# Row sums of a 64 MB array: loads of 16 rows a partition in three buffers, a tapering last load, and a last row summed in three chained two-stream VectorE sums

## The chip, the cores and the metric

The kernel runs on one core of a Trainium2 chip. The metric is device time in microseconds (us). The span of a profile is shorter than that time by about 1.7 us: it goes from the first to the last instruction. All runs told here are of the fast state (granted clock 1.000).

## The reference

```python
def setup_inputs():
    batch, seq, dim = 32, 512, 1024
    return {"x": np.random.randn(batch, seq, dim).astype(np.float32)}

def reference(x):
    return np.sum(x, axis=-1).astype(np.float32)
```

That is 16,384 rows of 4 KB: 67.1 MB in, 64 KB out. Each of the 128 partitions gets 128 neighbouring rows (512 KB).

## The kernel before

The rows of a partition are loaded in 16 tiles of 8 rows (32 KB a partition, 4 MB in all) into four buffers. VectorE sums the first four rows of a tile in one instruction; ScalarE sums the other four with one copy and its accumulator each. The last tile comes in eight loads of one row, and the engines take turns. The code, cut to its core:

```python
    G = 8
    T = C // G                       # C = 128 rows a partition, T = 16 tiles
    DVE_N = 4
    x_t = x_flat.rearrange("(p t j) d -> t p j d", p=P, j=G)
    xpool = ctx.enter_context(tc.tile_pool(name="x", bufs=4))
    # ... res: one fp32 column a row, 128 x 128
    for t in range(T):
        xt = xpool.tile([P, G, D], x.dtype, tag="xt")
        c0 = t * G
        if t < T - 1:
            nc.sync.dma_start(out=xt, in_=x_t[t])
            reduce_cols_dve(xt[:, 0:DVE_N], c0, DVE_N)      # one tensor_reduce
            for j in range(DVE_N, G):
                reduce_col_act(xt[:, j], c0 + j)            # Copy with accum_out, in place
        else:
            for j in range(G):
                nc.sync.dma_start(out=xt[:, j], in_=x_t[t, :, j])
            for j in range(G):
                if j % 2 == 0:
                    reduce_col_act(xt[:, j], c0 + j)
                else:
                    reduce_cols_dve(xt[:, j], c0 + j, 1)
    nc.sync.dma_start(out=out2d, in_=res)
```

Of the kernel before, what the change touches and what calls it, by code (L numbers as in the profile page):

```python
# [1 line left out]

# [4 lines left out]


@with_exitstack
def kernel(  # L10
    ctx: ExitStack,
    tc: tile.TileContext,
    x: bass.AP,
    out: bass.AP,
):
    nc = tc.nc
    P = nc.NUM_PARTITIONS

    x_flat = x.flatten_outer_dims()
    R, D = x_flat.shape  # L20
    assert R % P == 0
    C = R // P

    G = 8
    assert C % G == 0
    T = C // G
    DVE_N = 4

    x_t = x_flat.rearrange("(p t j) d -> t p j d", p=P, j=G)

    out2d = out.rearrange("a (b c) -> (a b) c", c=C)

    xpool = ctx.enter_context(tc.tile_pool(name="x", bufs=4))
    rpool = ctx.enter_context(tc.tile_pool(name="res", bufs=1))

    res = rpool.tile([P, C], mybir.dt.float32)

    def reduce_col_act(xt_col, c):
        nc.scalar.activation(  # L39
            out=xt_col,  # L40
            in_=xt_col,
            func=mybir.ActivationFunctionType.Copy,
            accum_out=res[:, c : c + 1],
        )

    def reduce_cols_dve(xt_cols, c0, n):
        nc.vector.tensor_reduce(  # L47
            out=res[:, c0 : c0 + n],
            in_=xt_cols,
            axis=mybir.AxisListType.X,  # L50
            op=mybir.AluOpType.add,
        )

    for t in range(T):
        xt = xpool.tile([P, G, D], x.dtype, tag="xt")
        c0 = t * G
        if t < T - 1:
            nc.sync.dma_start(out=xt, in_=x_t[t])  # L58
            reduce_cols_dve(xt[:, 0:DVE_N], c0, DVE_N)
            for j in range(DVE_N, G):  # L60
                reduce_col_act(xt[:, j], c0 + j)
        else:
            for j in range(G):
                nc.sync.dma_start(out=xt[:, j], in_=x_t[t, :, j])
            for j in range(G):
                if j % 2 == 0:
                    reduce_col_act(xt[:, j], c0 + j)
                else:
                    reduce_cols_dve(xt[:, j], c0 + j, 1)

    nc.sync.dma_start(out=out2d, in_=res)


# [1 line left out]
_INS = ['x']  # L75
_OUTS = [((32, 512), 'float32')]


# [23 lines left out]
```

## Time and profile before

| | before |
|---|---|
| time, median | 165.24 us (165.18 to 165.28) |
| span of the profile | 163.7 us |
| VectorE, ScalarE busy | 43%, 43% |
| DMA in the chain of waits (the work that ended last, followed back) | 88% |
| last load lands, last row sum ends | 160.02, 161.26 us |

The page of the kernel before. The DMA row has one digit for each of 40 slices of the span, the mean busy share of the 16 DMA engines in tenths.

```profile
span 163.7 us, 243 instructions
DVE 71.0 (43%) x19; ACT 69.6 (43%) x129; POOL 0.2 (0%) x4
...
DMA  6999999999999999999999999999999999998980
...
DMA packets 3457, 67.18 MB, mean 410 GB/s; under 512 B 384, under 2 KB 512, under 8 KB 1536
```

The DMA engines are busy nearly all the time and the two summing engines less than half of it. So work on those engines costs time only where no load can hide it, which is at the end.

The timeline of the kernel before, VectorE alone. Columns: start, duration, engine, line, operation, output<-input, shapes, and in brackets the idle time before it and what ended that.

```profile
120.72 4.42 DVE L47 TENSOR_REDUCE res<-xt 128x4 f32<-128x4096 f32 x1 [5.30 <-DMA xt<-in_x_dram]
130.43 4.42 DVE L47 TENSOR_REDUCE res<-xt 128x4 f32<-128x4096 f32 x1 [5.29 <-DMA xt<-in_x_dram]
140.14 4.42 DVE L47 TENSOR_REDUCE res<-xt 128x4 f32<-128x4096 f32 x1 [5.29 <-DMA xt<-in_x_dram]
...
160.04 1.22 DVE L47 TENSOR_REDUCE res<-xt 128x1 f32<-128x1024 f32 x1 [1.28 <-DMA xt<-in_x_dram]
```

A load has landed when the last of the 16 DMA engines has marked its part of it complete. Each sum starts when its load has landed, so these starts are a clock for the stream: 9.71 us for 4,194,304 bytes is 432 GB/s. The last line is the tail: one row sum of 1.22 us after the last landing, and only then can the results be stored.

Below, a run of so many KB is the contiguous stretch that a load moves for one partition; each load has 128 runs, 8 for each DMA engine. The same kernel in two stretches, one with 32 KB runs and one with the 4 KB runs of the last tile. The last two columns are the DMA share and GB/s.

```profile
100.00:140.00 40.00, 17.68 (x4) 17.07 (x32) 0.00 (x0) 1.00 1.00 430
...
150.00:158.00 8.00, 6.99 (x4) 7.41 (x14) 0.00 (x0) 1.00 1.03 410
```

The DMA engines are equally busy in both, but move 5% less with the short runs. That is what a fixed cost for each run looks like.

### The profile page before, as it was taken

The page shows a single profiled execution, that of the slowest core. Times are in us where ns is not written, and L with a number is a line of the kernel's source. Part 1 is how long each engine was busy: PE and PEld are TensorE (multiplying, and loading weights), DVE is VectorE, ACT ScalarE, POOL GpSimd, SP SyncE. Part 2 cuts the span into 40 slices and gives each one's busy share as a digit, 9 for nine tenths or more (in the row PEclk, how much of TensorE's full clock was granted, in tenths as well). Part 3 has the DMA queues.
Part 4 walks back from the last instruction along what each step waited for, and adds up shares of the span by engine and source line. Part 5 has one row for each costly group of instructions (what it writes and reads, how often), then busy time and mean ns, then how long its engine had stood idle before and what let it go on. Part 6 is the DMA issues. An engine that isn't in the chain of part 4 may idle for free.

```text
span 163.7 us, 243 instructions
## 1 busy us (share of the span) xinstructions
DVE 71.0 (43%) x19; ACT 69.6 (43%) x129; POOL 0.2 (0%) x4
## 2 busy tenths in 40 slices
DVE  0006337091551907337090642808245190733952
ACT  3006337091551907336091642808145190733960
POOL 0000000000000000000000000000000000000000
DMA  6999999999999999999999999999999999998980
GB/s 200 432 432 440 416 448 416 416 432 424 424 424 440 416 448 424 416 456 424 432 442 416 448 416 424 448 432 432 432 424 448 416 424 448 424 432 364 407 349 16
DMA packets 3457, 67.18 MB, mean 410 GB/s; under 512 B 384, under 2 KB 512, under 8 KB 1536
## 3 DMA queue, kind: packets, MB, share of 16 engines
q1 hardware_dynamic: 3456, 67.18, 96.5%
q14 instruction: 1, 0.01, 0.0%
HBM read 67.11 MB, written 0.07 MB: 410 GB/s over the span
## 4 chain that ended last, share of the span: by engine, by line
DMA 88%; DVE 9%; SPq 1%; issue 0%
DMA xt<-in_x_dram 88%; DVE res L47 9%; SPq L58 1%
## 5 line engine op out<-in xcount | busy, mean ns | idle before, releaser
L47 DVE TENSOR_REDUCE res<-xt 128x4 f32<-128x4096 f32 (+1 forms) x19 | 71.0, 3745 | 90.3 <-DMA xt<-in_x_dram 90.3
L39 ACT ACTIVATE xt<-xt 128x1024 f32<-128x1024 f32 x64 | 66.8, 1044 | 89.6 <-DMA xt<-in_x_dram 89.6
L39 ACT ACTIVATION_READ_ACCUMULATOR xt<-xt 128x1 f32 x64 | 11.9, 187 | 0.0
L39 ACT ACT_TABLE_LOAD x1 | 1.3, 1283 | 0.7 <-PEq L86 0.7
L86 POOL MEMSET const-bfloat16-1.0<- 128x1 bf16 x1 | 0.1, 101 | 0.0
L86 POOL MEMSET const-uint8-127<- 128x1 uint8 x1 | 0.1, 101 | 0.0
L86 POOL MEMSET const-float32-0.0<- 128x1 f32 x1 | 0.1, 98 | 0.2 <-issue 0.2
L86 POOL MEMSET const-float32-1.0<- 128x1 f32 x1 | 0.1, 98 | 0.0
## 6 DMA issues: line engine op xcount, KB each, us to landing
xt<-in_x_dram SPq DMA_DIRECT2D x15, 4096.0 KB, 34.4
xt<-in_x_dram SPq DMA_DIRECT2D x8, 512.0 KB, 27.0
out_dram<-res SPq DMA_DIRECT2D x1, 64.0 KB, 1.5
```

Of the source, the lines that this page charges most:

```text
L39: nc.scalar.activation(out=xt_col, in_=xt_col, func=mybir.ActivationFunctionType.Copy, accum_out=res[:, c : c + 1],)
L47: nc.vector.tensor_reduce(out=res[:, c0 : c0 + n], in_=xt_cols, axis=mybir.AxisListType.X, op=mybir.AluOpType.add,)
L58: nc.sync.dma_start(out=xt, in_=x_t[t])
L86: nc = _bacc.Bacc("TRN2", target_bir_lowering=False, num_devices=1)
```

## The change

The intent is to shorten the stream by making its runs longer (64 KB), to let the last loads shrink by halves so that the engines keep up, and to shorten what is left after the last landing. A two-stream sum takes the two halves of a piece as two operands, adds them element by element and accumulates, so it takes in two elements at a time (a row sum of 1024 elements took 1.22 us). Its start value can be the result of the sum before, which chains the pieces of the last row. The diff, cut to its core:

```diff
-    G = 8
+    G = 16
-    xpool = ctx.enter_context(tc.tile_pool(name="x", bufs=4))
+    xpool = ctx.enter_context(tc.tile_pool(name="x", bufs=3))
+    part = rpool.tile([P, 4], F32, name="part")
+    def load(xt, c0, a, b):
+        nc.sync.dma_start(out=xt[:, a:b], in_=x_p[:, c0 * D + a : c0 * D + b])
+    def pairs_dve(xt, a, b, first, acc):
+        h = (b - a) // 2
+        nc.vector.tensor_tensor_reduce(
+            out=xt[:, a : a + h], in0=xt[:, a : a + h], in1=xt[:, a + h : b],
+            scale=1.0, scalar=first, op0=ADD, op1=ADD, accum_out=acc)
+    for t in range(T - 1):
+        ...
+        load(xt, c0, 0, G * D)
+        rows_dve(xt, c0, 0, G // 2)             # 8 rows in one tensor_reduce
+        rows_act(xt, c0, G // 2, G // 2)        # 8 rows, one by one
+    c0 = (T - 1) * G
+    ...
+    for n in (8, 4, 2, 1):
+        load(xt, c0, j * D, (j + n) * D)
+        ...
+    cuts = [j * D + k for k in (0, D // 2, 3 * D // 4, D)]
+    for a, b in zip(cuts, cuts[1:]):
+        load(xt, c0, a, b)
+    # each of the runs of 8, 4, 2 rows: half to VectorE, half to ScalarE; the single row to ScalarE
+    acc = [part[:, 0:1], part[:, 1:2], res[:, C - 1 : C]]
+    for i, (a, b) in enumerate(zip(cuts, cuts[1:])):
+        pairs_dve(xt, a, b, acc[i - 1] if i else 0.0, acc[i])
```

Rows are counted from 0 below: the single row is row 14 of the last tile, and the last row is row 15.

More of the change, by code (lines that the diff above doesn't have):

```diff
@@ L6 @@
 from concourse._compat import with_exitstack
+F32 = mybir.dt.float32
+ADD = mybir.AluOpType.add
 @with_exitstack
@@ L22 @@
     C = R // P
-    G = 8
+    x_p = x_flat.rearrange("(p c) d -> p (c d)", p=P)
+    out2d = out.rearrange("a (b c) -> (a b) c", c=C)
+    G = 16
     assert C % G == 0
     T = C // G
-    DVE_N = 4
-    x_t = x_flat.rearrange("(p t j) d -> t p j d", p=P, j=G)
-    out2d = out.rearrange("a (b c) -> (a b) c", c=C)
-    xpool = ctx.enter_context(tc.tile_pool(name="x", bufs=4))
+    xpool = ctx.enter_context(tc.tile_pool(name="x", bufs=3))
     rpool = ctx.enter_context(tc.tile_pool(name="res", bufs=1))
-    res = rpool.tile([P, C], mybir.dt.float32)
@@ L38, in reduce_col_act @@
-    def reduce_col_act(xt_col, c):
-        nc.scalar.activation(
-            out=xt_col,
-            in_=xt_col,
-            func=mybir.ActivationFunctionType.Copy,
-            accum_out=res[:, c : c + 1],
-        )
-    def reduce_cols_dve(xt_cols, c0, n):
-        nc.vector.tensor_reduce(
-            out=res[:, c0 : c0 + n],
-            in_=xt_cols,
-            axis=mybir.AxisListType.X,
-            op=mybir.AluOpType.add,
-        )
-    for t in range(T):
-        xt = xpool.tile([P, G, D], x.dtype, tag="xt")
+    res = rpool.tile([P, C], F32, name="res")
@@ new lines, with rows_dve, rows_act @@
+    part = rpool.tile([P, 4], F32, name="part")
+    def load(xt, c0, a, b):
+        nc.sync.dma_start(out=xt[:, a:b], in_=x_p[:, c0 * D + a : c0 * D + b])
+    def rows_dve(xt, c0, j, n):
+        nc.vector.tensor_reduce(
+            out=res[:, c0 + j : c0 + j + n],
+            in_=xt[:, j * D : (j + n) * D].rearrange("p (j d) -> p j d", d=D),
+            axis=mybir.AxisListType.X,
+            op=ADD,
+        )
+    def rows_act(xt, c0, j, n):
+        for i in range(j, j + n):
+            v = xt[:, i * D : (i + 1) * D]
+            nc.scalar.activation(
+                out=v,
+                in_=v,
+                func=mybir.ActivationFunctionType.Copy,
+                accum_out=res[:, c0 + i : c0 + i + 1],
+            )
@@ L56 @@
+    def pairs_dve(xt, a, b, first, acc):
+        h = (b - a) // 2
+        nc.vector.tensor_tensor_reduce(
+            out=xt[:, a : a + h],
+            in0=xt[:, a : a + h],
+            in1=xt[:, a + h : b],
+            scale=1.0,
+            scalar=first,
+            op0=ADD,
+            op1=ADD,
+            accum_out=acc,
+        )
+    for t in range(T - 1):
         c0 = t * G
-        if t < T - 1:
-            nc.sync.dma_start(out=xt, in_=x_t[t])
-            reduce_cols_dve(xt[:, 0:DVE_N], c0, DVE_N)
-            for j in range(DVE_N, G):
-                reduce_col_act(xt[:, j], c0 + j)
-        else:
-            for j in range(G):
-                nc.sync.dma_start(out=xt[:, j], in_=x_t[t, :, j])
-            for j in range(G):
-                if j % 2 == 0:
-                    reduce_col_act(xt[:, j], c0 + j)
-                else:
-                    reduce_cols_dve(xt[:, j], c0 + j, 1)
+        xt = xpool.tile([P, G * D], F32, tag="xt", name="xt")
+        load(xt, c0, 0, G * D)
+        rows_dve(xt, c0, 0, G // 2)
+        rows_act(xt, c0, G // 2, G // 2)
@@ new lines @@
+    c0 = (T - 1) * G
+    xt = xpool.tile([P, G * D], F32, tag="xt", name="xt")
+    j = 0
+    runs = []
+    for n in (8, 4, 2, 1):
+        load(xt, c0, j * D, (j + n) * D)
+        runs.append((j, n))
+        j += n
+    cuts = [j * D + k for k in (0, D // 2, 3 * D // 4, D)]
+    for a, b in zip(cuts, cuts[1:]):
+        load(xt, c0, a, b)
+    for j, n in runs:
+        if n > 1:
+            rows_dve(xt, c0, j, n // 2)
+            rows_act(xt, c0, j + n // 2, n // 2)
+        else:
+            rows_act(xt, c0, j, 1)
```

## The prediction

> **What bounds the kernel now.** The load stream. On the page DMA is at 0.9 or more in nearly every slice, VectorE and ScalarE at 43% each; the chain of waits is 88% "DMA xt", 9% VectorE. On the timeline loads of 4 MB land every 9.71 us (VectorE starts at 120.72, 130.43, 140.14, 149.86): 432 GB/s. The Trainium skill, "DMA: Bandwidth & Descriptors", section "Where 436 GB/s comes from", puts the ceiling at 435.2 GB/s; the trace agrees, and the plateau has 0.7% left. Around it lie a head (first landing at 13.55 us, 3.8 us more than its bytes need) and a tail: the last piece lands near 160.0, one VectorE row sum takes 1.22 us, the store and the end 2.4 us more, to 163.7.
>
> **What the change does.**
> 1. Runs of 64 KB, not 32 KB. In the stretches view, 150 to 158 us (4 KB runs) moves 410 GB/s against 432. Per DMA engine (a sixteenth) that is 160 ns a 4 KB run and 1214 ns a 32 KB run: an estimated fixed 9 ns a run. Before, an engine handles 15x8 runs of 32 KB and 8x8 of 4 KB, 184; after, 7x8 of 64 KB and 7x8 smaller, 112. If a 64 KB run is one packet, 72x9 ns = 0.65 us leave the stream; if it is cut in two, 0.15 us. All on the critical path. The single packet gets two chances in three: 0.5 us on average.
> 2. Three buffers of 8 MB, not four of 4 MB. A tile's work takes 8x1.10 = 8.8 us on VectorE, about 8.4 us on ScalarE, a load 19.4 us. Two loads (39 us) stay queued meanwhile: no starving, no gain.
> 3. Tapered tail. Each half run's work (4.4, 2.2, 1.2 us) ends before the next piece lands: no backlog. The last ScalarE row lands some 1.3 us before the end, needs 1.06+0.19 us, and is hidden.
> 4. Two-stream sums of the last row. A row sum of 1024 takes 1.21 us: about 0.15 us fixed, 1 element a cycle; two streams halve the cycles. Estimates: 256 pairs 0.42 us, 128 pairs 0.28 us, plus an accumulator read of perhaps 0.1 us (ScalarE's takes 0.19). The three sums are chained by their start value and their data lands 0.33 us apart, less than a sum with read and wait needs, so the chain runs behind: I expect the last sum to end 0.8 us after the last landing, where it was 1.29: 0.5 us gained, on the critical path.
>
> Head, store and launch cost (165.22 less 163.7) stay.
>
> **Predicted time.** 165.22 - 0.5 - 0.5 = 164.2, say 164.1 us; 163.4 to 164.9 at 8 in 10. Faster by over 2%: 2%; within 2%: 97%; slower by over 2%: 1%. Nothing here gives 3.3 us: the stream itself is 155 us.
>
> **What the profile would show.** Step 1: about 2,200 packets in place of 3,457 (3,100 if cut), landings 19.40 us apart rather than 19.42. Step 2: queue waits on VectorE of over 8 us, no hole in the DMA row. Step 3: ScalarE ends before VectorE's last sum. Step 4: the chain of waits ends in short sums of 0.25 to 0.45 us, 0.6 to 1.1 us from last landing to last sum.
>
> **What would make it wrong.** 64 KB runs moving slower; DMA engines drifting further apart with larger runs, so that landings wait for the slowest; runs of 1 and 2 KB costing far more than 9 ns each; a two-stream sum or its read costing several times my estimate, three times in a row; the last ScalarE row ending last.

## The result

| | before | after |
|---|---|---|
| time, median | 165.24 us | 164.06 us (163.96 to 164.19) |
| span of the profile shown | 163.7 us | 162.4 us |
| packets | 3457 | 2161 |
| spacing of landings, for 8 MB | 19.42 us (120 to 140 us) | 19.35 us (100 to 139 us) |
| last sum ends | 161.26 us | 159.86 us |

The ratio is 0.9934 (95% interval 0.992 to 0.9948). A ratio is the mean time of one kernel's fast runs over that of the other's of the same rounds, so it is not quite the ratio of the medians. Two later calls, on two chips, gave 0.9937 and 0.9931. So the gain is about 1.1 us. The two profiled spans differ by 1.3 us, but the kernel before had spans of 163.2 to 163.6 us in its later executions: its profiled one was on the long side.

The page of the changed kernel:

```profile
span 162.4 us, 220 instructions
DVE 69.9 (43%) x16; ACT 69.0 (43%) x129; POOL 0.2 (0%) x4
...
DMA  7979989989989989989997997997997997999980
GB/s 258 517 323 452 517 355 420 517 371 404 501 355 436 517 371 404 517 371 404 517 452 325 517 468 307 517 468 323 501 484 323 484 484 307 452 420 408 418 350 20
DMA packets 2161, 67.18 MB, mean 414 GB/s; under 512 B 240, under 2 KB 624, under 8 KB 880
```

Each 64 KB run is one packet. 7x128 of them, 128 for each of the four larger pieces and 128 for each of the three smaller ones, 128 for the store, one for each of 16 engines and 15 DMAs that marks its completion, and one instruction fetch make 896+512+384+128+240+1 = 2161. A run cut in two would have given 896 more.

The sevens in the DMA row are not holes in the stream. The GB/s row jumps between 307 and 517, well above and below what the loads can do. A 64 KB packet takes more than half of a 4 us slice (2.42 us in the packet records), and the jumps are what counting each packet whole in one slice would give. The evenly spaced landings decide.

The timeline of the changed kernel, VectorE alone, three sums of the plateau, 19.36 and 19.35 us apart (the earlier spacings of this trace are 19.30 to 19.69 us):

```profile
100.73 8.69 DVE L43 TENSOR_REDUCE res<-xt 128x8 f32<-128x8192 f32 x1 [10.72 <-DMA xt<-in_x_dram]
120.09 8.69 DVE L43 TENSOR_REDUCE res<-xt 128x8 f32<-128x8192 f32 x1 [10.67 <-DMA xt<-in_x_dram]
139.44 8.69 DVE L43 TENSOR_REDUCE res<-xt 128x8 f32<-128x8192 f32 x1 [10.66 <-DMA xt<-in_x_dram]
```

And the end of the same timeline, with ScalarE and the store:

```profile
157.83 1.06 ACT L53 ACTIVATE xt<-xt 128x1024 f32<-128x1024 f32 x1
158.64 0.42 DVE L62 CUSTOM_DVE_ANT_0 xt<-xt 128x256 f32<-128x256 f32 x1 [0.87 <-DMA xt<-in_x_dram]
158.79 0.19 ACT L53 ACTIVATION_READ_ACCUMULATOR xt<-xt 128x1 f32 x1
158.99 0.08 DVE L62 DVE_READ_ACCUMULATOR2_ANT part<- 128x1 f32 x1
159.11 0.35 DVE L62 CUSTOM_DVE_ANT_0 xt<-xt,part 128x128 f32<-128x128 f32 x1
159.38 0.08 DVE L62 DVE_READ_ACCUMULATOR2_ANT part<- 128x1 f32 x1
159.50 0.35 DVE L62 CUSTOM_DVE_ANT_0 xt<-xt,part 128x128 f32<-128x128 f32 x1
159.78 0.08 DVE L62 DVE_READ_ACCUMULATOR2_ANT res<- 128x1 f32 x1
159.93 0.35 SPq L102 DMA_DIRECT2D out_dram<-res  x1
```

Only the first of the three sums has an idle time ended by a load. The other two follow with a gap of 0.04 to 0.05 us, so their data was there already. ScalarE finishes at 158.98, 0.9 us before the last sum.

The chain of waits of the changed kernel, where it meets the first two sums (start, duration, what):

```profile
111.36 47.10 DMA xt<-in_x_dram
158.47 0.03 issue
158.49 0.05 DVEq L62
158.54 0.10 issue
158.64 0.21 DVE xt L62
```

The chain leaves the loads at 158.47, when the half row lands. From there to the end of the last read (159.86) it holds nothing but the three sums, their reads and the issue between them. So the two quarter rows are hidden behind the sums, and not the other way round. The semaphore records of the kept trace, which no view above prints, have the quarter rows landing at 158.80 and 159.12 us: the last read ends 0.74 us after the last landing, where it was 1.24 us in the kernel before (160.02 to 161.26).

### The profile page after: what moved, and what is told of

It reads as the page before. It is cut to its first block, busy times and chain, and to the rows that moved or that the text cites. A ratio compares the mean times of both kernels' runs of the same rounds, so it can differ in the third digit from the quotient of the medians.

```text
span 162.4 us, 220 instructions
## 1 busy us (share of the span) xinstructions
DVE 69.9 (43%) x16; ACT 69.0 (43%) x129; POOL 0.2 (0%) x4
## 2 busy tenths in 40 slices
DMA packets 2161, 67.18 MB, mean 414 GB/s; under 512 B 240, under 2 KB 624, under 8 KB 880
## 4 chain that ended last, share of the span: by engine, by line
DMA 85%; DVE 11%; SPq 1%; issue 1%; DVEq 0%
DMA xt<-in_x_dram 85%; DVE res L43 11%; SPq L40 1%; DVE xt L62 0%; DVE part L62 0%; DVEq L62 0%; DVEq L128 0%
## 5 line engine op out<-in xcount | busy, mean ns | idle before, releaser
L43 DVE TENSOR_REDUCE res<-xt 128x8 f32<-128x8192 f32 (+3 forms) x10 | 68.7, 6873 | 89.0 <-DMA xt<-in_x_dram 89.0
L62 DVE CUSTOM_DVE_ANT_0 xt<-xt,part 128x128 f32<-128x128 f32 x2 | 0.7, 352 | 0.1
```

What stands on the lines that cost most here:

```text
L43: nc.vector.tensor_reduce(out=res[:, c0 + j : c0 + j + n], in_=xt[:, j * D : (j + n) * D].rearrange("p (j d) -> p j d", d=D), axis=mybir.A ...
L62: nc.vector.tensor_tensor_reduce(out=xt[:, a : a + h], in0=xt[:, a : a + h], in1=xt[:, a + h : b], scale=1.0, scalar=first, op0=ADD, op1=A ...
```

## The experiments

The kernel before had medians of 165.05 to 165.24 us. Ratios are against the kernel before in the same call, so kernels of different calls are compared by them.

Theory A, that of the prediction, has two parts: every run costs a DMA engine a fixed 9 ns, so that fewer runs shorten the stream; and the last row's sum after the last landing is 0.5 us shorter. Rival B says that run size does nothing and the whole gain is the tail. Rival C says that the whole gain is the stream. A further rival lays part of it on the buffers.

| run | ratio (95% interval) | median, us |
|---|---|---|
| changed kernel | 0.9937 (0.9925 to 0.995) | 164.07 |
| long runs, old tail | 0.9974 (0.9962 to 0.9987) | 164.56 |
| old runs, new tail | 0.9976 (0.9963 to 0.9988) | 164.53 |
| changed, runs cut to 32 KB | 0.9977 (0.9963 to 0.999) | 164.66 |
| changed, runs cut to 8 KB | 1.014 (1.0126 to 1.0153) | 167.47 |
| changed, plain last row | 0.9967 (0.9954 to 0.9979) | 164.62 |
| changed, one two-stream sum | 0.9945 (0.9932 to 0.9959) | 164.21 |
| changed, last row in halves | 0.9929 (0.9916 to 0.9941) | 163.95 |
| changed kernel, third chip | 0.9931 (0.9917 to 0.9945) | 164.00 |
| halves, third chip | 0.9926 (0.9914 to 0.9939) | 163.93 |
| six chained sums (wrong result) | 1.0007 (0.9994 to 1.0019) | 165.19 |
| changed, two buffers | 0.9939 (0.9927 to 0.9952) | 164.08 |

### The changed kernel again

No edit.

> The changed kernel itself, for comparison on this chip. Every theory: 164.1 us against 165.2, span near 162.4.

Measured: 164.07 us, span 162.1 us, as expected. Its landings are 19.34 to 19.36 us apart from 42.46 us on.

### Long runs, old tail

```diff
-    # pieces of 8, 4, 2, 1, 1/2, 1/4, 1/4 rows and chained sums
+    load(xt, c0, 0, G // 2 * D)
+    for j in range(G // 2, G):
+        load(xt, c0, j * D, (j + 1) * D)
+    rows_dve(xt, c0, 0, G // 4)
+    rows_act(xt, c0, G // 4, G // 4)
+    # then the 8 single rows by ScalarE and VectorE in turn
```

> 64 KB runs and three buffers kept, but the end of the kernel before (8 rows in one load, then 8 single rows, each summed by one engine). Theory A (each run costs an engine a fixed 9 ns, so fewer runs shorten the stream, and the last row's sum gains 0.5 us): an engine handles 128 runs against 184 before, 56x9 ns = 0.5 us; the end after the last landing stays 1.29 us; so 164.6 to 164.8 us. Rival B (the run size does nothing, the whole gain comes from the tail): 165.2. Rival C (the whole gain comes from the stream): 164.1.

Measured: 164.56 us, ratio 0.9974. About 0.4 us of the gain remains and 0.5 to 0.6 us is gone. Rival B (165.2) and rival C (164.1) both fail.

### Old runs, new tail

```diff
-    G = 16
+    G = 8
-    bufs=3
+    bufs=4
-    for n in (8, 4, 2, 1):
+    for n in (4, 2, 1):
```

> The kernel before with 4 MB tiles of 32 KB runs and four buffers; only the tail is new (last tile in pieces of 4, 2, 1 rows, 1/2, 1/4, 1/4, the last row in chained two-stream sums). Theory A: 112+56 = 168 runs an engine against 184, 0.14 us, and 0.5 us from the last sum: 164.6 us. Rival B: 164.1. Rival C: 165.1.

Measured: 164.53 us, ratio 0.9976. With the run before, this makes a two-by-two table of runs and tail: long runs alone gain 0.26%, the new tail alone 0.24%, both together 0.63%. The two gains add up to 0.50%, or 0.8 us against 1.04 us; each carries an interval of 0.2 us either way, so they add up within what can be told apart.

### The changed kernel with 32 KB runs

```diff
-        load(xt, c0, 0, G * D)
+        for k in range(2):
+            load(xt, c0, k * G * D // 2, (k + 1) * G * D // 2)
```

> The changed kernel with each 64 KB load cut into two loads of 32 KB runs, tiles and buffers kept. Theory A: 56 more runs an engine at 9 ns, 0.5 us slower than the changed kernel: 164.6 us, packets near 3,170, the same as the run with only the new tail; then the number and size of the buffers do nothing. If the three larger buffers matter by themselves, this one stays near 164.1 and the run with only the new tail does not.

Measured: 164.66 us and 3,169 packets, 0.59 us slower than the changed kernel on the same chip, where 0.5 us was expected. It equals the run with four small buffers and the same number of runs (0.9977 and 0.9976). So the tile size and the buffers do nothing that shows. The cost goes with the number of runs, or with the number of loads, which was the same in these two kernels as well; the next section comes back to this.

### The changed kernel with 8 KB runs

The same edit with 8 in place of 2.

> The changed kernel with each 64 KB load cut into eight loads of 8 KB runs, to enlarge the disputed cost. Theory A: 7x56 = 392 more runs an engine at 9 ns, 3.5 us slower than the changed kernel: 167.6 us. Rival B: no change, 164.1.

Measured: 167.47 us with 9,218 packets, 3.4 us slower than the changed kernel; expected was 167.6. The spacing of landings shows the same cost without the tail in it. From the timelines, VectorE alone, first the changed kernel again, then the one with 32 KB runs, then the one with 8 KB runs:

```profile
61.81 8.69 DVE L43 TENSOR_REDUCE res<-xt 128x8 f32<-128x8192 f32 x1 [10.66 <-DMA xt<-in_x_dram]
81.16 8.69 DVE L43 TENSOR_REDUCE res<-xt 128x8 f32<-128x8192 f32 x1 [10.67 <-DMA xt<-in_x_dram]
```

```profile
52.37 8.69 DVE L43 TENSOR_REDUCE res<-xt 128x8 f32<-128x8192 f32 x1 [10.74 <-DMA xt<-in_x_dram]
71.79 8.69 DVE L43 TENSOR_REDUCE res<-xt 128x8 f32<-128x8192 f32 x1 [10.74 <-DMA xt<-in_x_dram]
```

```profile
52.91 8.69 DVE L43 TENSOR_REDUCE res<-xt 128x8 f32<-128x8192 f32 x1 [11.20 <-DMA xt<-in_x_dram]
72.79 8.69 DVE L43 TENSOR_REDUCE res<-xt 128x8 f32<-128x8192 f32 x1 [11.19 <-DMA xt<-in_x_dram]
```

For the same 8 MB that is 19.35, 19.42 and 19.88 us. An engine handles 8, 16 and 64 runs in that time. The steps are 0.07 us for 8 runs and 0.46 us for 48 runs: 9 and 10 ns a run.

No run tested one rival. Every load here has eight runs an engine, so these edits add loads and runs together, and the cost could lie with the load. The packet records of the changed kernel's kept trace, which no view prints one by one, decide it. Their median time is 159 ns for 4 KB, 611 ns for 16 KB, 1,213 ns for 32 KB and 2,418 ns for 64 KB: two packets of 32 KB take 8 ns more than one of 64 KB. The packet by which an engine marks a load complete takes 9 ns. Eight 64 KB packets and one mark make 19.35 us, the spacing itself. So one more load of eight runs costs an engine an estimated 8x8 + 9 = 73 ns, nearly all of it for the runs, and the 9 ns a run are 8 ns with the run's share of the mark. The fixed cost is settled from 4 KB to 64 KB. Without it, 32,768 B in 1,205 ns an engine make 435 GB/s for 16 engines.

### A plain last row

```diff
-    cuts = [j * D + k for k in (0, D // 2, 3 * D // 4, D)]
+    cuts = [j * D + k for k in (0, D)]
-    # three chained pairs_dve
+    rows_dve(xt, c0, G - 1, 1)
```

> The changed kernel with the last row in one load and one ordinary VectorE row sum. Theory A: the last landing comes some 0.14 us earlier (16 runs fewer an engine), the sum then takes 0.05+1.22 us against 0.78 us: 0.35 us slower than the changed kernel, 164.4 us. If the split and the two-stream sums gained nothing: 164.0.

Measured: 164.62 us, ratio 0.9967 against 0.9934 for the changed kernel: 0.5 us slower, where 0.35 was expected. I had credited it with a last landing that comes 0.14 us earlier for having two pieces fewer. The semaphore records show about half of it. From the landing of the single row before to the last landing it took 1.23 us here and 1.22 us in the next kernel, both with one piece, 1.27 us with two pieces, and 1.31 us in the changed kernel with its three; why not more stays open. From this kernel's timeline, VectorE alone:

```profile
158.99 1.22 DVE L43 TENSOR_REDUCE res<-xt 128x1 f32<-128x1024 f32 x1 [1.30 <-DMA xt<-in_x_dram]
```

The sum ends 1.24 us after the last landing (158.97), against 0.74 us in the changed kernel.

### One two-stream sum

```diff
-    cuts = [j * D + k for k in (0, D // 2, 3 * D // 4, D)]
+    cuts = [j * D + k for k in (0, D)]
-    acc = [part[:, 0:1], part[:, 1:2], res[:, C - 1 : C]]
+    acc = [res[:, C - 1 : C]]
```

> The changed kernel with the last row in one load and one two-stream sum of 512 pairs, no chain. From the trace of the changed kernel: start 0.17 us after the landing, 0.43 us for 256 pairs plus 256 more at 1 a cycle, so 0.69 us, and the accumulator read to 0.05 us past its end: 0.91 us after a landing that comes 0.14 us earlier. So within 0.1 us of the changed kernel: the cut into three pieces and the chain are worth nothing beyond the two-stream sum. If the cut into pieces is what gains: 164.4.

Measured: 164.21 us, ratio 0.9945. That is 0.1% or some 0.2 us behind the changed kernel, where at most 0.1 was expected, and 0.4 us ahead of the plain row. From its timeline, VectorE alone:

```profile
159.11 0.69 DVE L62 CUSTOM_DVE_ANT_0 xt<-xt 128x512 f32<-128x512 f32 x1 [1.44 <-DMA xt<-in_x_dram]
159.72 0.08 DVE L62 DVE_READ_ACCUMULATOR2_ANT res<- 128x1 f32 x1
```

The 0.69 us were as expected: 0.87 us from the landing at 158.93 to the end of the read, between the 1.24 us of the plain row and the 0.74 us of the changed kernel. Most of the tail's gain is thus the second stream. The three pieces and their chain add little, and the intervals do not separate the two kernels.

### The last row in halves

```diff
-    cuts = [j * D + k for k in (0, D // 2, 3 * D // 4, D)]
+    cuts = [j * D + k for k in (0, D // 2, D)]
-    acc = [part[:, 0:1], part[:, 1:2], res[:, C - 1 : C]]
+    acc = [part[:, 0:1], res[:, C - 1 : C]]
```

> The changed kernel with the last row in two halves, so two chained sums instead of three. In the trace of the changed kernel the chain starts 0.17 us after the half row's landing and then runs through without a wait for data, 1.40 us from that landing to the last read. One link fewer: start 0.17, 0.43, gap 0.05, 0.45, read 0.05: 1.1 us from the first half's landing, about 0.3 us faster than the changed kernel, 163.8 us. If the chain is not what paces the end but the last landing is: no more than 0.1 us faster.

Measured: 163.95 us, ratio 0.9929: 0.1 us faster than the changed kernel at best, not 0.3. From its timeline, VectorE alone:

```profile
158.47 0.42 DVE L62 CUSTOM_DVE_ANT_0 xt<-xt 128x256 f32<-128x256 f32 x1 [0.87 <-DMA xt<-in_x_dram]
158.82 0.08 DVE L62 DVE_READ_ACCUMULATOR2_ANT part<- 128x1 f32 x1
159.06 0.48 DVE L62 CUSTOM_DVE_ANT_0 xt<-xt,part 128x256 f32<-128x256 f32 x1 [0.15 <-DMA xt<-in_x_dram]
159.47 0.08 DVE L62 DVE_READ_ACCUMULATOR2_ANT res<- 128x1 f32 x1
```

The second sum now has an idle time ended by a load, at 158.92. I had left out that with one link fewer the last landing takes over: a gain from shortening a chain goes only as far as the next thing that ends late. The last sum ends 0.63 us after that landing.

### Halves beside the changed kernel

No edit to the version with halves.

> The version with the last row in two halves again, beside the changed kernel on one chip. Its trace showed the second sum waiting 0.15 us for the last landing and ending 0.63 us after it, where the chain of three ended 0.78 us after an estimated landing. So about 0.15 us faster than the changed kernel, less than the intervals can show; the trace's last sum should end 0.60 to 0.66 us after the last landing.

Measured: 163.93 us (163.72 to 164.03) beside 164.00 us (163.96 to 164.21) for the changed kernel, whose expectation was:

> The changed kernel once more, as the comparison on this chip: 0.993 to 0.994 of the kernel before.

The ratios are 0.9926 and 0.9931. The sign is the same in both and the size is within the noise. In this trace no wait is put down to the last landing, but the semaphore records have it: the first half landed at 158.48, the last at 159.07, and the first sum's read ended at 159.08, a tie. The last read ended at 159.70, 0.63 us after the last landing, as expected. Halves are the best version that I ran, though its lead over the changed kernel is not shown to be more than noise.

### Six chained sums

```diff
+    sums = [j * D + k for k in (0, D // 4, D // 2, 5 * D // 8, 3 * D // 4, 7 * D // 8, D)]
-    for i, (a, b) in enumerate(zip(cuts, cuts[1:])):
+    for i, (a, b) in enumerate(zip(sums, sums[1:])):
```

> All loads of the changed kernel, the same last row summed in six chained sums instead of three (each piece cut in two). If the chain of sums sets the end: a sum of 64 pairs takes about 0.29 us and follows its predecessor after about 0.33 us, a sum of 128 pairs after 0.39 us; start as before, then 0.36+0.39+4x0.33 = 2.07 us instead of 1.22 us: 0.8 us slower than the changed kernel, 164.9 us. If the landings set the end: no more than 0.1 us slower, as the last piece has then only one sum of 64 pairs more to do.

This run failed by my mistake. The name `j` holds 14 at that place, not 15, so the six sums took row 14 once more and the result was wrong (relative error 0.12). They waited for ScalarE's copy of row 14 instead of the last pieces. So it doesn't decide whether chain or landings set the end in the changed kernel; its time (165.19 us) is no test of that. What it does show is the price of a link when the data is long there. From its timeline, VectorE alone:

```profile
159.34 0.35 DVE L62 CUSTOM_DVE_ANT_0 xt<-xt,part 128x128 f32<-128x128 f32 x1
...
159.73 0.28 DVE L62 CUSTOM_DVE_ANT_0 xt<-xt,part 128x64 f32<-128x64 f32 x1
...
160.06 0.28 DVE L62 CUSTOM_DVE_ANT_0 xt<-xt,part 128x64 f32<-128x64 f32 x1
...
160.39 0.28 DVE L62 CUSTOM_DVE_ANT_0 xt<-xt,part 128x64 f32<-128x64 f32 x1
```

A link of 128 pairs takes 0.39 us from start to start, a link of 64 pairs 0.33 us. Halving the data saves 0.06 us of 0.39.

### Two buffers

```diff
-    bufs=3
+    bufs=2
```

> The changed kernel with two buffers instead of three. A buffer comes free 8.8 us after its landing and the other load lasts 19.4 us, so the stream still has over 10 us of queued bytes when the next load is issued: 164.1 us, as the changed kernel. If the three buffers are needed to keep the stream full: a hole at every load, several us slower.

Measured: 164.08 us, ratio 0.9939 beside 0.9931, within the intervals. Even the third buffer isn't needed. Its queue waits 125.2 us in all on VectorE, but each load is issued while the other one still runs.

## Why the prediction was right

The time (164.1 predicted, 164.06 measured) and both terms of the sum held.

1. **Long runs.** Right, and the single packet that I gave two chances in three is what happened: 2,161 packets against "about 2,200". Long runs alone gained 0.4 us (old tail), and taking them away from the changed kernel cost 0.6 us, around the 0.5 us of 56 runs at 9 ns. The fixed cost held up to 8 KB runs at 9 to 10 ns. Luck had a part in the closeness: the 164.1 us average the two cases and round 164.2 down. With the single packet taken as sure, the prediction's own terms give 165.22 - 0.65 - 0.5 = 164.07 us. One figure was a slip: I wrote landings 19.40 us apart rather than 19.42, but 8 runs fewer at 9 ns give 19.35, which is what the undisturbed spacings have.
2. **Buffers.** Right. Two, three or four buffers of two sizes made no difference. The longest wait of a load's issue for a buffer that VectorE still read was 29.6 us, while the two queued loads ran.
3. **Tapered tail.** Right as far as no backlog formed: each sum of the taper starts with an idle time ended by a load, and ScalarE ends 0.9 us before the last sum. That the taper itself gains anything over single rows isn't shown: the old tail and the taper with a plain last row gave 0.9974 and 0.9967, with overlapping intervals.
4. **The last row.** The size was right: 0.5 us. The last read ended 0.74 us after the last landing, where 0.8 was predicted, and 1.24 us in the kernel before, where the prediction had 1.29: both 0.05 us less, so the difference held. The pieces landed 0.33 and 0.32 us apart, as predicted, and the chain did run behind the data. Of its parts, 256 pairs (0.42) fit, while 128 pairs with a start value took 0.35 us and not 0.28, and a two-stream sum starts 0.17 us after a landing where a row sum starts 0.02 us after it; a shorter read (0.08 for 0.1) and an overlap of the read with the sum made up for that.

The Trainium skill, "VectorE: DVE Perf Modes", gives fp32 `tensor_tensor` as (N+151)/0.96 ns in its section "The TRN2 errata — SBUF-src ops pay a fixed extra latency per instruction". By estimate from that formula it is 424 ns for 256 and 691 ns for 512; the two-stream sums without a start value agree (0.42 and 0.69 us), although they accumulate as well.

What stays open: most traces have a spacing of landings that is 0.15 to 0.35 us too long, not always at the same place (9.95 us among 9.7 in the kernel before, 19.69 in the changed one), and the changed kernel run again has none. The packet records show where the time goes: in the changed kernel's first trace eight 64 KB packets that began between 40 and 42 us took 2.49 to 2.89 us, where the median is 2.42 us, and in the kernel before 44 packets of 32 KB that began between 34 and 42 us took 1.26 to 1.39 us, where the median is 1.21 us. What slows them no run here tells; it is part of the scatter of the times. Why two-stream sums start later after a landing is open too.

## What to carry to other kernels

Where a kernel is one long stream of loads, count the runs an engine handles and multiply by the cost of one: at the 9 ns measured here, marks included, this bounds the gain before any code is written, and here it was 0.4% because the runs were long already. At the end of such a stream only what ends after the last landing counts, and a chain of small instructions is paid by the link (0.33 us here even for 64 pairs), so two pieces did no worse than three. When a link is removed, look for what ends next: here the last landing took over and left 0.1 us of an expected 0.3.

## What the Trainium skill lacked or had wrong

- "DMA: Bandwidth & Descriptors", section "Why small descriptors are slow (HBM only)", names a fixed overhead of about 3 cycles a packet, works it out for 256 B, and gives no cost for runs of 4 KB and more. Here the fixed cost is 8 ns a packet from 4 KB to 64 KB and 9 ns for the packet that marks a load complete, 9 to 10 ns a run together by the landings.
- The same page, section "Where 436 GB/s comes from", says that the HBM side (about 358 GB/s) binds transfers between HBM and SBUF, and beside it calls a measured 425 GB/s near fabric rate. The page's note under its measured table keeps the one-core case apart; read alone, the section misleads for it. The one core here came to 433 GB/s (8,388,608 bytes in 19.35 us), and its packets to 435 GB/s without their fixed cost, which agrees with the ports' 435 GB/s and not with 358.
- The same page's rule of at least 1 MiB a DMA for 75% of the peak doesn't say that queued loads can do with less: loads of 512 KB, queued behind others, kept 410 GB/s. No run here has such a load on its own.
- "VectorE: DVE Perf Modes" doesn't have the two-stream sum with accumulator: (N+151)/0.96 ns fits it, a start value read from SBUF adds 0.06 us (0.42 to 0.48 us for 256 pairs), its accumulator read takes 0.08 us, and it starts 0.17 us after a landing against 0.02 us for a row sum.
